# 16x16 blocks gathered on chip for a block inverse, and norm sums moved ahead of their products, in a hybrid decoder layer

## The chip, the cores and the metric

The kernel runs on one core of a Trainium2 chip. The metric is the device time of one execution in microseconds, as the median of several runs. A core has a matrix engine (TensorE, PE in the rows; PEld is its loading of the stationary operand), a vector engine (VectorE, DVE), an engine for functions and scaled copies (ScalarE, ACT), a general one (GpSimd, Pool), and a queue engine (SyncE, SP) that issues transfers. Every engine works its own instructions in order; they wait for one another through semaphores. A "q" behind an engine's name in a row is its sequencer, which waits or issues. Transfers are issued from SP, ACT and Pool.

## The reference

One layer on a sequence of 256 tokens, with 2048 channels. An input projection feeds three token mixers, their outputs are mixed and projected, and a SwiGLU FFN follows, each with a norm before and a norm after:

```
h = rms_norm(x, norm_mix_pre)
p = h @ w_in                                     # columns for three mixers and the merge gates
y_a = RG-LRU(p)     y_b = gated DeltaNet(p)      y_c = RWKV-7(p)
m = sum_b sigmoid(gate_b) * (y_b @ w_branch[b])
x = x + rms_norm(m @ w_out, norm_mix_post)
h = rms_norm(x, norm_ffn_pre)
x = x + rms_norm((silu(h @ w_gate) * (h @ w_up)) @ w_down, norm_ffn_post)
```

DeltaNet (8 heads, chunks of 64 tokens) and RWKV-7 (16 heads) are written in chunked form, and each chunk needs the inverse of a unit triangular 64x64 matrix.

## The kernel before

Products are made in three parts: each factor is split into a rounded high part and the rest, and high x high, high x low and low x high are added up. The weights arrive as tiles of 1 MB (`raw`, L203, issued from SP, three buffers); each half of one is cast to `wh` on ACT (L214) and the rest `wl = raw - wh` is made on DVE (L216), three buffers each; then TensorE multiplies (L241 to L243 or L262 to L264). The order of instructions on each engine is laid down before the run by a planner that simulates the engines; `high_priority` and `issue_after` steer it.

The mixers run in four quarters of 256 channels. A quarter `q` projects the slabs of RWKV (`rwkv_quarter`), of DeltaNet (`gdn_pair`) and of the LRU (`lru_quarter`). The first two make the triangular matrices of their chunks, `st` (L564, 1 MB) and `U` (L750, 0.25 MB), and hand them to `inverse64`, which works in steps:

- The 16x16 blocks on the diagonals are copied from SBUF to a DRAM tile `dblk`, with eight transfers issued from Pool (L381), one for each group of 16 partitions `r`.
- They come back in one transfer from Pool (L383) into the SBUF tile `B`, in which each of the 16 partitions of a group holds all the blocks of its group: 8 KB per partition for RWKV (`nu` = 8), 4 KB for DeltaNet (`nu` = 4), so 1 MB and 0.5 MB. The source has dimensions 8, 16 (repeated) and the row.
- `after = yield` returns to the caller, who goes on with DeltaNet and the LRU. When the LRU's last instruction (L867) is known, `xc` is set (L388) behind it, and a recurrence of 15 steps on DVE (L392, L393) inverts the 16x16 blocks out of `B`.
- Small products on TensorE join 16 to 32 and 32 to 64 (L410 to L435), and the rest of the mixer follows.

Meanwhile TensorE has the next quarter's projections. Behind the last quarter come the remaining gate blocks and `branch(0)`, whose inputs `yf`, `yh`, `yl` (L1030 to L1033) take buffers of the tag `u4`, which `B` of DeltaNet has too (there are six).

`product_a` makes the output projection and the last projection of the FFN, in four column blocks `j` for two halves `t` of the tokens. Each result is squared and summed on ACT (L1090) and multiplied by the norm's weight on DVE (L1091). Behind `product_a` the sums are reduced (L1105, L1167), `rstd` scales them on DVE (L296) and takes the power -1/2 on Pool (L297), and the residual is added: in `group` (L1110), and in the end for `j` < 3 on DVE (L1173), for `j` = 3 as a scaled copy on ACT (L1175) and an add on Pool (L1176); each part is then written out (L1177).

Of the kernel before, what the change touches and what calls it, by code (L numbers as in the profile page):

```python
# [8 lines left out]
F32 = mybir.dt.float32  # L9
# [5 lines left out]
P = 128  # L15
# [125 lines left out]
class Builder:  # L141
# [227 lines left out]
    def inverse64(self, nu, diag16, block, transposed):  # L369
# [4 lines left out]


        dd = self.dp.tile([8, nu, 16, 16], F32, name=self.uid("dblk"))
        for r in range(8):
            src = diag16(r)
            dst = dd[r].rearrange("(u n) j t -> j u n t", n=src.shape[2]) if len(src.shape) == 4 else \
                dd[r].rearrange("u j t -> j u t")  # L380
            nc.gpsimd.dma_start(dst, src)  # L381
        B = (self.u8 if nu == 8 else self.u4)("B").rearrange("p (u j t) -> p u j t", u=nu, j=16)
        nc.gpsimd.dma_start(B.rearrange("p u j t -> p (u j t)"),  # L383
                            dd.rearrange("r u j t -> r (u j t)").unsqueeze(1).to_broadcast([8, 16, nu * 256]))
# [72 lines left out]
    def rwkv_quarter(self, q, kS, rS, vS, up, y):  # L457
# [110 lines left out]
        X, = yield from self.inverse64(8, lambda r: st8[16 * r:16 * r + 16, :, (r < 4)::2, 16 * r:16 * r + 16],  # L568
# [128 lines left out]
    def gdn_pair(self, q_, qS, kS, vS, sz, y):  # L697
# [70 lines left out]
        J, JT = yield from self.inverse64(4, lambda r: h4(U)[16 * r:16 * r + 16, :, 16 * r:16 * r + 16],  # L768
# [103 lines left out]
def build(tc, aps, out):  # L872
# [209 lines left out]
    def product_a(w, ah, al, kts, hm, nw, ssq):  # L1082
        for j in range(4):
            b.ahead_evac = FIRST if j == 3 else None
            js = slice(j * 512, (j + 1) * 512)

            def sink(ps, j=j, js=js):
                for t in range(2):
                    junk = sp.tile([P, 512], F32, name=b.uid("junk"), tag="stage", bufs=b.stage_bufs)
                    nc.scalar.activation(junk, ps[t], AF.Square, accum_out=ssq[:, t, j:j + 1])  # L1090
                    nc.vector.tensor_tensor(hm[:, t, js], ps[t], nw[:, js], ALU.mult)  # L1091

            b.block_a(wp, pp, w[j], ah, al, kts, sink, j == 3)
        b.ahead_evac = None
# [3 lines left out]
    product_a(aps["w_out"], mh, ml, KD, hm, n2, ssq)  # L1098
    x1d = [b.dp.tile([P, D], F32, name=f"x1d{t}") for t in range(2)]
    xh, xl = acts("h")  # L1100
    with tc.high_priority(FIRST):
        tots = [fp.tile([P, 6], F32, name=f"tot{t}") for t in range(2)]
        r1 = []
        for t in range(2):
            nc.vector.tensor_reduce(tots[t][:, 0:1], ssq[:, t], AX.X, ALU.add)  # L1105
            r1.append(b.rstd(fp, tots[t][:, 0:1], 1, 1.0 / D, EPS))

        def group(t, k0):
            js = slice(k0 * P, (k0 + 4) * P)
            nc.vector.scalar_tensor_tensor(x1[t][:, js], hm[:, t, js], r1[t], x1[t][:, js], ALU.mult, ALU.add)  # L1110
            return x1[t][:, js]

        last = b.to_channels(pp, group, "n3", xh, xl)
# [49 lines left out]
    product_a(aps["w_down"], ah, al, KF, od, n4, ssq)  # L1163
    r4 = []
    for t in range(2):
        tot = ap_.tile([P, 1], F32, name=f"tot4{t}")
        nc.vector.tensor_reduce(tot, ssq[:, t], AX.X, ALU.add)  # L1167
        r4.append(b.rstd(ap_, tot, 1, 1.0 / D, EPS))
    for t in range(2):
        for j in range(4):  # L1170
            js = slice(j * 512, (j + 1) * 512)
            if j < 3:
                nc.vector.scalar_tensor_tensor(od[:, t, js], od[:, t, js], r4[t], x1[t][:, js], ALU.mult, ALU.add)  # L1173
            else:
                nc.scalar.activation(od[:, t, js], od[:, t, js], AF.Identity, scale=r4[t])  # L1175
                nc.gpsimd.tensor_tensor(od[:, t, js], od[:, t, js], x1[t][:, js], ALU.add)  # L1176
            (nc.sync, nc.scalar)[j % 2].dma_start(out[t * P:(t + 1) * P, js], od[:, t, js])  # L1177
# [22 lines left out]
```

## Time and profile before

| | us |
|---|---|
| time, median of 3 runs (1879.31 to 1880.51) | 1879.42 |
| profiled execution | 1879.03 |
| its span, first to last instruction | 1877.3 |
| TensorE busy | 1839.9 |
| DVE busy | 1114.8 |
| ACT busy | 850.5 |
| Pool busy | 82.6 |

The table's busy times are of the profiled execution. A matmul's end is modelled, so a stretch with TensorE busy throughout is one in which its queue did not run dry. The granted clock is a share of full speed (1.00 is 2.4 GHz, 0.50 is 1.2 GHz). The share of transfers is the mean busy share of the 16 transfer engines. In a row of the time line the columns are the start, the duration, the engine, the line of the program, the operation, what it writes and reads, the shapes, how many are merged into the row, and in brackets the idle time before it and what ended that.

### The profile page before, as it was taken

The page shows a single profiled execution, that of the slowest core. Times are in us where ns is not written, and L with a number is a line of the kernel's source. Part 1 is how long each engine was busy: PE and PEld are TensorE (multiplying, and loading weights), DVE is VectorE, ACT ScalarE, POOL GpSimd, SP SyncE. Part 2 cuts the span into 40 slices and gives each one's busy share as a digit, 9 for nine tenths or more (in the row PEclk, how much of TensorE's full clock was granted, in tenths as well). Part 3 has the DMA queues.
Part 4 walks back from the last instruction along what each step waited for, and adds up shares of the span by engine and source line. Part 5 has one row for each costly group of instructions (what it writes and reads, how often), then busy time and mean ns, then how long its engine had stood idle before and what let it go on. Part 6 is the DMA issues. An engine that isn't in the chain of part 4 may idle for free.

```text
span 1877.3 us, 27855 instructions
## 1 busy us (share of the span) xinstructions
PE 1839.9 (98%) x11516; PEld 1591.6 (85%) x11516; DVE 1114.8 (59%) x1622; ACT 850.5 (45%) x1055; POOL 82.6 (4%) x150
## 2 busy tenths in 40 slices
PE   9999999999999999899999999999999999999997
PEld 9999997999798988677888887888888888888886
DVE  6768667666776577656655556445545444444444
ACT  7445355434543465334444445444444444443442
POOL 0011010200120012000000000000000000000000
PEclk9999999999999999899999999999999999999999
DMA  7565445644565355648655556555555555555553
GB/s 263 183 183 200 141 152 189 169 162 153 178 168 175 134 183 174 202 164 310 209 194 183 195 186 234 194 196 184 194 187 191 191 181 199 204 200 188 194 200 114
DMA packets 61647, 352.06 MB, mean 188 GB/s; under 512 B 9040, under 2 KB 10832, under 8 KB 22480
## 3 DMA queue, kind: packets, MB, share of 16 engines
q1 hardware_dynamic: 50256, 327.18, 50.4%
q10 hardware_dynamic: 6752, 14.31, 2.1%
q0 software_dynamic: 4512, 8.79, 1.9%
q8 instruction: 90, 1.47, 0.3%
q14 instruction: 37, 0.30, 0.0%
HBM read 336.22 MB, written 14.02 MB: 187 GB/s over the span
## 4 chain that ended last, share of the span: by engine, by line
PE 53%; issue 38%; DMA 4%; DVE 3%; ACT 2%; POOL 1%; ACTq 0%; DVEq 0%; POOLq 0%; SPq 0%
PE mm L264 8%; PE mm L263 8%; PE mm L262 8%; PE mm L243 7%; PE mm L242 7%; PE mm L241 7%; DMA raw<-in_w_in_dram 2%; DVE wl L216 1%; DMA B<-dblk 1%; ACT wh L214 1%; PE psa L592 1%; PE pr L585 1%; PE pr L596 1%; PE px L562 0%; PE pst L602 0%
## 5 line engine op out<-in xcount | busy, mean ns | idle before, releaser
L216 DVE TENSOR_TENSOR wl<-raw,wh 128x1024 fp32r<-128x1024 f32 x590 | 720.9, 1223 | 616.8 <-ACT wh L214 614.6
L214 ACT CAST wh<-raw 128x1024 fp32r<-128x1024 f32 x590 | 620.1, 1052 | 856.9 <-PE mm L264 594.8
L241 PE MATMUL mm<-xh,wh 128*128 128x256 f32 x1200 | 344.4, 287 | 5.3 <-ACT wh L214 5.3
L243 PE MATMUL mm<-xh,wl 128*128 128x256 f32 x1200 | 344.9, 288 | 2.1 <-DVE wl L216 1.1
L242 PE MATMUL mm<-xl,wh 128*128 128x256 f32 x1200 | 345.0, 288 | 1.1 <-DVE xl L909 1.0
L263 PE MATMUL mm<-wl,hh 128*128 128x512 f32 x704 | 275.1, 391 | 0.5 <-DVE wl L216 0.5
L264 PE MATMUL mm<-wh,hl 128*128 128x512 f32 x704 | 274.8, 390 | 0.0
L262 PE MATMUL mm<-wh,hh 128*128 128x512 f32 x704 | 250.7, 392 | 2.0 <-DVE rstd L296 1.5
L241 PEld LDWEIGHTS mm<-xh,wh 128*128 128x128 f32 x1200 | 232.2, 194 | 7.5 <-ACT wh L214 6.0
L243 PEld LDWEIGHTS mm<-xh,wl 128*128 128x128 f32 x1200 | 231.9, 193 | 3.9 <-DVE wl L216 1.7
L242 PEld LDWEIGHTS mm<-xl,wh 128*128 128x128 f32 x1200 | 232.1, 193 | 2.4 <-DVE xl L909 1.5
L262 PEld LDWEIGHTS mm<-wh,hh 128*128 128x128 f32 x704 | 132.3, 188 | 29.4 <-ACT hh L311 2.5
L263 PEld LDWEIGHTS mm<-wl,hh 128*128 128x128 f32 x704 | 132.7, 189 | 27.8 <-DVE wl L216 0.7
L264 PEld LDWEIGHTS mm<-wh,hl 128*128 128x128 f32 x704 | 132.6, 188 | 27.5
L263 PE MATMUL mm<-wl,xh 128*128 128x512 f32 x384 | 151.0, 393 | 1.2 <-DVE wl L216 1.1
L264 PE MATMUL mm<-wh,xl 128*128 128x512 f32 x384 | 150.2, 391 | 0.0
L262 PE MATMUL mm<-wh,xh 128*128 128x512 f32 x384 | 139.5, 392 | 0.0
L263 PE MATMUL mm<-wl,ah 128*128 128x512 f32 x352 | 137.0, 389 | 0.0
L264 PE MATMUL mm<-wh,al 128*128 128x512 f32 x352 | 136.9, 389 | 0.0
L262 PE MATMUL mm<-wh,ah 128*128 128x512 f32 x352 | 123.5, 389 | 0.0
L297 POOL TENSOR_TENSOR rstd<-rstd,mhalf 128x8 f32<-128x8 f32 (+3 forms) x23 | 29.7, 1295 | 1453.7 <-DVE rstd L296 1453.7
L263 PEld LDWEIGHTS mm<-wl,xh 128*128 128x128 f32 x384 | 72.1, 188 | 17.8 <-DVE wl L216 2.5
(294 smaller groups left out, 2023.8 us busy)
## 6 DMA issues: line engine op xcount, KB each, us to landing
raw<-in_w_in_dram SPq DMA_DIRECT2D x72, 1024.0 KB, 4.9
raw<-in_w_mix_dram SPq DMA_DIRECT2D x48, 1024.0 KB, 4.9
raw<-in_w_gate_dram SPq DMA_DIRECT2D x44, 1024.0 KB, 4.9
raw<-in_w_up_dram SPq DMA_DIRECT2D x44, 1024.0 KB, 4.8
raw<-in_w_down_dram SPq DMA_DIRECT2D x44, 1024.0 KB, 4.9
raw<-in_w_branch_dram SPq DMA_DIRECT2D x24, 1024.0 KB, 4.9
raw<-in_w_out_dram SPq DMA_DIRECT2D x16, 1024.0 KB, 4.8
keep<-stage ACTq DMA_DIRECT2D x24, 256.0 KB, 5.2
```

What stands on the lines that cost most here:

```text
L214: nc.scalar.copy(wh[:, :n], s)
L216: nc.vector.tensor_tensor(wl[:, :n], s, wh[:, :n].bitcast(F32), ALU.subtract)
L241: nc.tensor.matmul(o, hs, xh[:, k], start=(k == 0 and c == 0), stop=False, skip_group_check=True)
L242: nc.tensor.matmul(o, hs, xl[:, k], start=False, stop=False, skip_group_check=True)
L243: nc.tensor.matmul(o, ls, xh[:, k], start=False, stop=(k == kts - 1), skip_group_check=True)
L262: nc.tensor.matmul(ps[t], xh[:, k, ts], h, start=(k == 0), stop=False)
L263: nc.tensor.matmul(ps[t], xh[:, k, ts], l, start=False, stop=False)
L264: return nc.tensor.matmul(ps[t], xl[:, k, ts], h, start=False, stop=(k == kts - 1))
L297: nc.gpsimd.tensor_tensor(r, r, self.mhalf.to_broadcast([P, n]), ALU.pow)
L585: nc.tensor.matmul(pq[bb, us], st[u][:, n, bb], sav[:, n, us], start=not n, stop=True, skip_group_check=True)
L592: nc.tensor.matmul(ps[bb, us], X[bb, 2 * u + p], R[bb, us], start=True, stop=True)
L596: nc.tensor.matmul(pq[ob, us], st[u][:, n, ob], sav[:, n, us], start=not n, stop=True, skip_group_check=True)
```

## The change

Three things are edited.

- `inverse64` no longer issues eight transfers. For each quarter of the partitions (32, two groups of 16) ACT copies the left block columns, multiplied by a 0/1 mask of the partitions, into an SBUF tile `C`, and DVE adds the right block columns times the other mask. One transfer from Pool writes `C` to `dblk`, and `B` is read from there, with the block's row `j` now ahead of the unit `u`. `C` uses the buffers of the tag that the recurrence's `xt` has.
- `product_a` takes a function `rms`, called for the last column block between the square and the weight product, that reduces the sums and makes `rstd`; both callers hand in theirs.
- At the end both the third and the fourth column block are scaled on ACT, and all four adds are on DVE; nothing is added on Pool.

```diff
@@ -366,22 +366,28 @@
             nc.vector.scalar_tensor_tensor(out[:, c], out[:, c], mu(c), s[:, c, 1:257], ALU.mult, ALU.add)
 
 
-    def inverse64(self, nu, diag16, block, transposed):
+    def inverse64(self, nu, diag, block, transposed):
 
 
 
         nc, mp, n = self.nc, self.mp, nu * 32
 
-        dd = self.dp.tile([8, nu, 16, 16], F32, name=self.uid("dblk"))
-        for r in range(8):
-            src = diag16(r)
-            dst = dd[r].rearrange("(u n) j t -> j u n t", n=src.shape[2]) if len(src.shape) == 4 else \
-                dd[r].rearrange("u j t -> j u t")
-            nc.gpsimd.dma_start(dst, src)
-        B = (self.u8 if nu == 8 else self.u4)("B").rearrange("p (u j t) -> p u j t", u=nu, j=16)
-        nc.gpsimd.dma_start(B.rearrange("p u j t -> p (u j t)"),
-                            dd.rearrange("r u j t -> r (u j t)").unsqueeze(1).to_broadcast([8, 16, nu * 256]))
+        def like(t, a):
+            return t.rearrange("p (u n) t -> p u n t", n=a.shape[2]) if len(a.shape) == 4 else t
+        C = mp.tile([P, nu, 16], F32, name=self.uid("C"), tag=f"xt{nu}", bufs=2)
+        for i in range(4):
+            qs = slice(32 * i, 32 * i + 32)
+            nc.scalar.activation(like(C[qs], diag(i, 0)), diag(i, 0), AF.Copy, scale=self.cst("blk16", 0, 1)[qs])
+            nc.vector.scalar_tensor_tensor(like(C[qs], diag(i, 1)), diag(i, 1), self.cst("blk16", 16, 1)[qs],
+                                           like(C[qs], diag(i, 1)), ALU.mult, ALU.add)
+        dd = self.dp.tile([P, nu * 16], F32, name=self.uid("dblk"))
+        nc.gpsimd.dma_start(dd, C.rearrange("p u t -> p (u t)"))
+        B = (self.u8 if nu == 8 else self.u4)("B")
+        nc.gpsimd.dma_start(B, dd.rearrange("(r j) n -> r (j n)", j=16).unsqueeze(1).to_broadcast([8, 16, nu * 256]))
+        B = B.rearrange("p (j u t) -> p u j t", u=nu, j=16)
         after = yield
         xc = mp.tile([P, nu, 16], F32, name=self.uid("xc"), tag=f"xc{nu}", bufs=1)
         with self.tc.issue_after(after):
@@ -565,7 +571,8 @@
                                         ps[h].rearrange("p (m e s) -> p m e s", m=2, e=2), mask, ALU.mult)
 
 
-        X, = yield from self.inverse64(8, lambda r: st8[16 * r:16 * r + 16, :, (r < 4)::2, 16 * r:16 * r + 16],
+        X, = yield from self.inverse64(8, lambda i, h: st8[32 * i:32 * i + 32, :, (i < 2)::2,
+                                                               32 * i + 16 * h:32 * i + 16 * h + 16],
                                        lambda h, w: st[w // 2][64 * h:64 * h + 64, 2 * (w % 2) + (h < 1),
                                                                64 * h:64 * h + 64], False)
 
@@ -765,7 +772,7 @@
             nc.scalar.activation(kd[:, i], h4(ps)[:, i], AF.Copy, scale=h4(dm)[:, 2 * i, P - 1:P])
 
 
-        J, JT = yield from self.inverse64(4, lambda r: h4(U)[16 * r:16 * r + 16, :, 16 * r:16 * r + 16],
+        J, JT = yield from self.inverse64(4, lambda i, h: h4(U)[32 * i:32 * i + 32, :, 32 * i + 16 * h:32 * i + 16 * h + 16],
                                lambda h, u: h4(U)[64 * h:64 * h + 64, u, 64 * h:64 * h + 64], True)
         lo_, hi = slice(0, 64), slice(64, 128)
         v64 = lambda t: t[:, 0:256].rearrange("p (u t) -> p u t", t=64)
@@ -1079,7 +1086,8 @@
         x1.append(fp.tile([P, D], F32, name=f"x1_{t}"))
         nc.scalar.dma_start(x1[t], aps["x"][t * P:(t + 1) * P])
 
-    def product_a(w, ah, al, kts, hm, nw, ssq):
+    def product_a(w, ah, al, kts, hm, nw, ssq, rms):
         for j in range(4):
             b.ahead_evac = FIRST if j == 3 else None
             js = slice(j * 512, (j + 1) * 512)
@@ -1088,6 +1096,8 @@
                 for t in range(2):
                     junk = sp.tile([P, 512], F32, name=b.uid("junk"), tag="stage", bufs=b.stage_bufs)
                     nc.scalar.activation(junk, ps[t], AF.Square, accum_out=ssq[:, t, j:j + 1])
+                    if j == 3:
+                        rms(t)
                     nc.vector.tensor_tensor(hm[:, t, js], ps[t], nw[:, js], ALU.mult)
 
             b.block_a(wp, pp, w[j], ah, al, kts, sink, j == 3)
@@ -1095,16 +1105,17 @@
 
     hm = fp.tile([P, 2, D], F32, name="hm")
     ssq = fp.tile([P, 2, 4], F32, name="ssq")
-    product_a(aps["w_out"], mh, ml, KD, hm, n2, ssq)
+    tots = [fp.tile([P, 6], F32, name=f"tot{t}") for t in range(2)]
+    r1 = []
+    def rms1(t):
+        nc.vector.tensor_reduce(tots[t][:, 0:1], ssq[:, t], AX.X, ALU.add)
+        r1.append(b.rstd(fp, tots[t][:, 0:1], 1, 1.0 / D, EPS))
+    product_a(aps["w_out"], mh, ml, KD, hm, n2, ssq, rms1)
     x1d = [b.dp.tile([P, D], F32, name=f"x1d{t}") for t in range(2)]
     xh, xl = acts("h")
     with tc.high_priority(FIRST):
-        tots = [fp.tile([P, 6], F32, name=f"tot{t}") for t in range(2)]
-        r1 = []
-        for t in range(2):
-            nc.vector.tensor_reduce(tots[t][:, 0:1], ssq[:, t], AX.X, ALU.add)
-            r1.append(b.rstd(fp, tots[t][:, 0:1], 1, 1.0 / D, EPS))
         def group(t, k0):
             js = slice(k0 * P, (k0 + 4) * P)
             nc.vector.scalar_tensor_tensor(x1[t][:, js], hm[:, t, js], r1[t], x1[t][:, js], ALU.mult, ALU.add)
@@ -1160,21 +1171,25 @@
     n4 = full(xp, "n4", aps["n4"], tag="xl")
     od = xp.tile([P, 2, D], F32, name="od", tag="xh")
     ssq = ap_.tile([P, 2, 4], F32, name="ssq2")
-    product_a(aps["w_down"], ah, al, KF, od, n4, ssq)
     r4 = []
-    for t in range(2):
+    def rms4(t):
         tot = ap_.tile([P, 1], F32, name=f"tot4{t}")
         nc.vector.tensor_reduce(tot, ssq[:, t], AX.X, ALU.add)
         r4.append(b.rstd(ap_, tot, 1, 1.0 / D, EPS))
+    product_a(aps["w_down"], ah, al, KF, od, n4, ssq, rms4)
     for t in range(2):
-        for j in range(4):
-            js = slice(j * 512, (j + 1) * 512)
-            if j < 3:
-                nc.vector.scalar_tensor_tensor(od[:, t, js], od[:, t, js], r4[t], x1[t][:, js], ALU.mult, ALU.add)
+        o = [od[:, t, j * 512:(j + 1) * 512] for j in range(4)]
+        x = [x1[t][:, j * 512:(j + 1) * 512] for j in range(4)]
+        for j in (3, 2):
+            nc.scalar.activation(o[j], o[j], AF.Identity, scale=r4[t])
+        for j in (0, 1, 3, 2):
+            if j < 2:
+                nc.vector.scalar_tensor_tensor(o[j], o[j], r4[t], x[j], ALU.mult, ALU.add)
             else:
-                nc.scalar.activation(od[:, t, js], od[:, t, js], AF.Identity, scale=r4[t])
-                nc.gpsimd.tensor_tensor(od[:, t, js], od[:, t, js], x1[t][:, js], ALU.add)
-            (nc.sync, nc.scalar)[j % 2].dma_start(out[t * P:(t + 1) * P, js], od[:, t, js])
+                nc.vector.tensor_tensor(o[j], o[j], x[j], ALU.add)
+            (nc.sync, nc.scalar)[j % 2].dma_start(out[t * P:(t + 1) * P, j * 512:(j + 1) * 512], o[j])
     while b.cp:
         b.drop()
```

## Rows read from the trace of the kernel before

**Rows 1.** The page: busy time of TensorE; the casts of weights on ACT.
```profile
PE 1839.9 (98%) x11516; PEld 1591.6 (85%) x11516; DVE 1114.8 (59%) x1622; ACT 850.5 (45%) x1055; POOL 82.6 (4%) x150
...
L214 ACT CAST wh<-raw 128x1024 fp32r<-128x1024 f32 x590 | 620.1, 1052 | 856.9 <-PE mm L264 594.8
```

**Rows 2.** Stretches: PE, PEld, DVE, ACT, POOL busy us; clock, transfer share, GB/s.
```profile
188.00:235.00 47.00, 47.00 (x675) 45.05 (x675) 29.46 (x85) 18.09 (x28) 0.00 (x0) 1.00 0.41 140
341.00:353.00 12.00, 12.00 (x100) 11.43 (x99) 9.34 (x15) 7.36 (x13) 8.98 (x17) 1.00 0.14 32
353.00:377.00 24.00, 21.36 (x176) 20.88 (x174) 15.66 (x30) 7.14 (x7) 0.60 (x1) 0.99 0.98 217
372.00:385.00 13.00, 10.04 (x59) 9.56 (x59) 8.93 (x31) 4.08 (x4) 0.00 (x0) 0.74 0.77 247
567.00:580.00 13.00, 9.53 (x57) 9.03 (x57) 8.31 (x29) 4.08 (x4) 0.00 (x0) 0.74 0.73 240
776.00:800.00 24.00, 18.08 (x377) 15.30 (x376) 12.75 (x53) 7.97 (x19) 0.00 (x0) 0.57 0.37 131
```

**Rows 3.** Time line of ACT and DVE, 374 to 378 us.
```profile
374.96 1.99 ACT L214 CAST wh<-raw 128x1024 fp32r<-128x1024 f32 x2 [8.65 <-DMA raw<-in_w_in_dram]
...
376.03 1.23 DVE L216 TENSOR_TENSOR wl<-raw,wh 128x1024 fp32r<-128x1024 f32 x1 [5.59 <-ACT wh L214]
```

**Rows 4.** Landing times, medians of the page; last, the weight load issued at 357.0.
```profile
raw<-in_w_in_dram SPq DMA_DIRECT2D x72, 1024.0 KB, 4.9
B<-dblk POOLq DMA_DIRECT2D x4, 1024.0 KB, 21.5
dblk<-U POOLq DMA_DIRECT2D x32, 4.0 KB, 2.4
...
DMA to landing us min/median/max: 17.8/17.8/17.8
```

**Rows 5.** Time line of Pool in the second and the fourth quarter.
```profile
343.43 4.10 POOL L381 DMA_DIRECT2D dblk<-U  x8 [28.86 <-DVE U L750]
...
351.80 0.62 POOL L383 DMA_DIRECT2D B<-dblk  x1
353.55 0.60 POOL L383 DMA_DIRECT2D B<-dblk  x1 [1.13 <-DMA dblk<-st]
...
742.38 4.17 POOL L381 DMA_DIRECT2D dblk<-st  x8 [1.04 <-DVE st L564]
...
748.41 0.60 POOL L383 DMA_DIRECT2D B<-dblk  x1 [1.25 <-DMA dblk<-st]
```

**Rows 6.** Instruction groups by shape: busy us and mean ns of one.
```profile
L437 ACT ACTIVATE XT<-px 32x128 f32<-32x128 f32 x8 | 2.1, 268 | 0.2
...
L611 DVE SCALAR_TENSOR_TENSOR S<-S,pc,cst_t 128x128 f32<-128x128 f32 x16 | 5.0, 345 | 0.1
```

**Rows 7.** Time line of DVE, 344 to 346 us.
```profile
344.60 1.29 DVE L564 TENSOR_TENSOR st<-px,cst_t 128x512 f32<-128x512 f32 x2 [0.54 <-PE px L562]
```

**Rows 8.** Time line of DVE and ACT, fourth quarter.
```profile
763.36 1.23 DVE L216 TENSOR_TENSOR wl<-raw,wh 128x1024 fp32r<-128x1024 f32 x1 [5.46 <-ACT wh L214]
...
779.37 1.05 ACT L1032 CAST yh<-yf 128x1024 fp32r<-128x1024 f32 x1 [1.16 <-DVE xt L392]
```

**Rows 9.** Time line of DVE between output projection and FFN.
```profile
1126.51 0.68 DVE L1091 TENSOR_TENSOR hm<-mm,n 128x512 f32<-128x512 f32 x1
...
1128.11 2.74 DVE L1110 SCALAR_TENSOR_TENSOR x<-hm,rstd,x 128x512 f32<-128x512 f32 x4 [0.67 <-POOL rstd L297]
```

**Rows 10.** Time line of DVE and ACT at the end.
```profile
1866.22 0.68 DVE L1091 TENSOR_TENSOR od<-mm,n 128x512 f32<-128x512 f32 x1
1866.82 0.14 DVE L1167 TENSOR_REDUCE tot<-ssq 128x1 f32<-128x4 f32 x1
...
1867.80 3.08 DVE L1173 SCALAR_TENSOR_TENSOR od<-od,rstd,x1r 128x512 f32<-128x512 f32 x3 [0.66 <-POOL rstd L297]
...
1865.82 0.19 ACT L1090 ACTIVATION_READ_ACCUMULATOR junk<-mm 128x1 f32 x1
```

## Prediction

> **What bounds the kernel now.** I read the page first. TensorE is busy for 1839.9 us of the span of 1877.3 [rows 1], so all that an edit can win is TensorE's idle time and the stretches in which its clock is low. Next I cut the span into stretches and read busy time and granted clock of each. In the first quarter's inverse TensorE has no idle time at all and the full clock, 2.4 GHz (188 to 235 us) [rows 2]. In the second and third quarter there is one hole each: 13 us hold 10.04 and 9.53 us of TensorE's work, at a mean clock of 0.74, so the clock was at its lower level (1.2 GHz) for 2 x 0.26 x 13 = 6.8 us [rows 2]. In the fourth (776 to 800) TensorE is busy 18.08 of 24 us at a mean clock of 0.57 [rows 2]. The other idle places are the passage between the output projection and the FFN, and the end.
>
> Then the waits: what made the hole of the second quarter? ACT waited 8.65 us for a weight tile from DRAM before two casts (L214), and DVE stood 5.59 us behind that cast although the inverse's recurrence (L392) was queued right after [rows 3]. So the hole is late weights. The transfers say why: a weight load of 1 MB lands in 4.9 us as a rule, the one issued at 357.0 took 17.8; the copy into B, also 1 MB, takes 21.5 [rows 4]. From 341 to 353 us the transfer engines are all but idle, share 0.14, and from 353 to 377 full, 0.98, at 217 GB/s [rows 2]. Pool's queue gives the order: U is there at 343.43, its eight gathers take 4.10 us to issue, the eight of st follow, and only then the two copies into B go out, at 351.80 and 353.55 [rows 5], into the time of the next weight loads. The gathers hold the B copies back through the idle time.
>
> **The change, part by part.** (a) The gather of the 16x16 blocks. Removed per inverse: seven of eight Pool issues, 8 inverses x 7 x 0.51 us (4.10 / 8 [rows 5]) = 29 us of Pool's time; on the path only the B copies are queued behind them. Added per inverse: four masked copies on ACT and four multiply-adds on DVE, each on 32 partitions of 128 or 64 elements, and one transfer on Pool. ACT's scaled copy of 32x128 took 0.27 us, DVE's three-operand form of 128x128 0.35 [rows 6]: 1.1 and 1.4 us per inverse, 8.6 and 11 us in all. In 188 to 235 us DVE is busy 29.5 and ACT 18.1 of 47 us while TensorE is full [rows 2], so I price these at nothing: TensorE's products cover them. Without that cover each inverse would cost 4 x 0.27 + 0.35 = 1.4 us.
>
> When do the B copies start? ACT's copies run ahead of DVE's adds, so the tile C stands 4 x 0.27 + 0.35 = 1.4 us after its source; then 0.5 us of issue and 2.4 of landing, the row of U's gathers [rows 4]: 4.3 us. U is there at 343.4 [rows 5]: its B copy goes out at 347.7 instead of 351.80. st is there at 345.9 [rows 7]: 350.2 instead of 353.55, 3.3 us earlier. If ACT is then in a cast (1.0 us) and DVE in a subtraction (1.2 us) [rows 3], it is 1.1 us earlier; those are the ends, and I take 3.3, since DVE has a gap of 0.54 us just there [rows 7].
>
> What does it give? The load that landed at 374.8 us (357.0 + 17.8 [rows 4]) stopped TensorE. It comes 3.3 us earlier by the shift. The 0.5 MB copy of U is also out of the crowded time then: 0.5 MB at 217 GB/s [rows 2] is 2.4 us more. TensorE lacked 13 - 10.04 = 2.96 us [rows 2], so 5.7 us of advance closes the hole with 2.7 to spare; the low end (1.1 + 2.4 = 3.5) just closes it too. Without the idle time I expect the clock to stay at 2.4 GHz, as in 188 to 235 us [rows 2]. Worth in the second quarter: 2.96 us idle, and half of the 6.8 us at 1.2 GHz, less some 0.75 of it that were idle: (6.8 - 0.75) / 2 = 3.0, together **6.0 us**. Third quarter: 3.47 idle and (6.8 - 1.1) / 2 = 2.8 [rows 2]: **6.3 us**. The first has no hole: nothing.
>
> Fourth quarter. st is there only at 742.4 and its copy goes out at 748.41 [rows 5]; afterwards at 742.4 + 4.3 = 746.7, 1.7 earlier, so this copy still meets weight loads. TensorE here is not short of weights alone: at the end of its idle time the cast of yh (L1032) waits for a buffer that the recurrence on B gives back, and the recurrence began behind a DVE subtraction that had waited 5.46 us for late weights [rows 8]. The weights come 1.7 + 2.4 = 4.1 us earlier by the same sum, and the chain behind with them: **4.1 us**. Its ends: 0, if the collision stays, and 5.5, the whole wait [rows 8]; with the clock full from 776 to 800 (2 x 0.43 x 24 = 20.6 us at 1.2 GHz [rows 2]) up to 10 more, which I leave out because TensorE's work there is a chain of small products with gaps.
>
> The Trainium skill, page "DMA: Bandwidth & Descriptors", section "Rules for kernel authors", says that a transfer whose outermost dimension is under 16 is confined to that many of the 16 engines. B's source begins with a dimension of 8 in both kernels. B's 21.5 us beside 4.9 for the same megabyte [rows 4] agrees, though other traffic is in that row. By this rule the costly copy stays as it is and only moves; that is the first rival.
>
> (b) Sums ahead of products at L1090. Between projection and FFN the second half's product into hm (L1091) starts on DVE at 1126.51, the reduction comes behind it, and the first residual add (L1110) at 1128.11 [rows 9]. Now the reduction goes first, and the product runs while Pool takes the power. One product holds the reduction for 0.60 us (1866.22 to 1866.82 at the end, which has the same pair [rows 10]): **0.6 us**. The ends are 0.3, if the product then stands before the add, and 0.7.
>
> (c) The end. Now: product 1866.22, reduction 1866.82, first of three adds 1867.80, and with Pool's add beside them the three take 3.08 us, to 1870.9 [rows 10]. Four adds without Pool took 2.74 [rows 9]. Pool's adds go, and DVE does four per half. The last sum is read at 1866.01 [rows 10]; the first half's adds, 0.6 us earlier and without Pool's company, are off DVE by then. From there 0.98 us to the first add, as from 1866.82 to 1867.80 [rows 10], and 2.74: 1869.7 instead of 1870.9, **1.1 us** with 0.1 for the hand-over. ACT's scaled copies go beside the first two adds. The ends are 0.4 and 1.4: an issue on ACT may stand before the square.
>
> The new order inside B (j before u) leaves the innermost run contiguous and L392's counts alike: nothing, under the cover named.
>
> Sum: 6.0 + 6.3 + 4.1 + 0.6 + 1.1 = 18.1 us. The profiled execution took 1879.03 us around its span of 1877.3; that gives 1860.9, and the median of the runs lies 0.4 above: **1861 us**.
>
> **The rivals.** *The collision only moves.* The B copies start 1 to 2 us earlier, since the masked copies wait behind casts and subtractions, and the weights still come late. For it: in the fourth quarter st itself is late [rows 5]; against it: twelve microseconds at share 0.14 [rows 2]. Then only (b) and (c) stay: 1879.4 - 1.7 = 1877.7 us. Chance 0.13.
>
> *The fourth quarter opens too.* 5.5 instead of 4.1, and 6 of the 10 us of low clock: 1861 - 1.4 - 6 = 1853.6 us. For it: the first quarter runs the same chain at full clock [rows 2]; against it: after 776 us few weight products are left to fill the gaps. Chance 0.14.
>
> *Slower: ACT is held.* ACT works in order. A masked copy that waits for U or st at the head of ACT holds the weight cast behind it, and DVE's add waits for ACT and holds the subtraction; DVE stood 5.59 us in that way [rows 3]. Place: 343 to 348 us and its likes, in all four quarters. It decides once ACT is held for longer than the split weights in stock last, three halves of some 3.2 us (590 casts in the span [rows 1]). Then a hole of 6 us stays in two quarters and appears in the two others: 1879.4 + 2 x 6 - 1.7 = 1890 us. Against it: the producers are done within some 2 us of each other [rows 5, 7]. Chance 0.07.
>
> **How the numbers follow.** The forecast has 0.66. On the low side the range takes in the better rival, with the ends of (b) and (c) and some of the remaining clock: 1849 us; on the high side one of the two holes kept and nothing from the fourth quarter: 1861 + 6.3 + 4.1 = 1871.4, 1872 us. Left out are the rival in which the collision only moves and the slower one, 0.20. Changes within 0.2% (3.8 us) can't be told from none here: faster by more 0.66 + 0.14 = 0.80, within 0.13, slower 0.07.
>
> **What would show it.** The B copy of st issued near 350 us, B's landing under 15 us; no wait of ACT for weights over 4 us in the middle quarters; TensorE full and at full clock where the two 13 us stretches are; the reduction ahead of hm's product; no Pool add at the end, and the last DVE add 1.1 us sooner after TensorE's last product. I am wrong if weight loads beside B still take 13 us and more, if casts stand behind masked copies that wait, or if the order of TensorE's work around the inverse is another one.

## The result, and the profile after

The changed kernel takes 1891.72 us (median of 4 runs, 1889.15 to 1892.20), the kernel before on the same chip 1879.37. The ratio is 1.0063, with a 95% interval of 1.0045 to 1.0080: **slower by 0.6%**, where 1861 us and faster was forecast.

| us | after |
|---|---|
| profiled execution, its span | 1889.15, 1887.4 |
| TensorE busy | 1840.8 |
| DVE, ACT, Pool busy | 1121.3, 864.4, 51.1 |

TensorE's work is the same (1839.9 before [rows 1]); the span is 10.1 us longer. To see where, one can match the 8880 weight products of both traces one by one and take the difference of their starts. After the first quarter's inverse they lag by 0.7 us, after the second's by 4.7, the third's 5.7, the fourth's 14.1; behind the passage to the FFN by 13.6; and the span ends 10.1 later. So in these two traces the gather costs 14.1 us, and the norm edits give 4.0 back. Such lags move by some 1 us from trace to trace where nothing was edited (norms_alone gains 1.2 us in the third quarter), so smaller differences of theirs say nothing.

What TensorE waits for has changed as well. Its first and third product of a weight tile, on the page of the kernel before and then on that of the kernel after:

```profile
L241 PE MATMUL mm<-xh,wh 128*128 128x256 f32 x1200 | 344.4, 287 | 5.3 <-ACT wh L214 5.3
L243 PE MATMUL mm<-xh,wl 128*128 128x256 f32 x1200 | 344.9, 288 | 2.1 <-DVE wl L216 1.1
```

```profile
L241 PE MATMUL mm<-xh,wh 128*128 128x256 f32 x1200 | 344.0, 287 | 0.0
L243 PE MATMUL mm<-xh,wl 128*128 128x256 f32 x1200 | 343.5, 287 | 13.0 <-DVE wl L216 13.0
```

Before, it waited for casts of late weights; after, for the weight subtractions on DVE.

The stretches of the holes in the kernel after (columns as in [rows 2]):

```profile
341.00:353.00 12.00, 12.00 (x98) 11.34 (x97) 10.05 (x23) 8.91 (x20) 1.78 (x3) 1.00 0.24 79
353.00:377.00 24.00, 16.84 (x137) 16.43 (x136) 14.61 (x24) 7.61 (x8) 0.61 (x1) 0.98 0.73 195
366.00:379.00 13.00, 7.28 (x51) 7.07 (x51) 4.22 (x15) 2.09 (x2) 0.00 (x0) 0.88 0.66 187
565.00:578.00 13.00, 7.51 (x49) 7.31 (x48) 6.17 (x22) 1.94 (x3) 0.00 (x0) 0.74 0.57 163
768.00:800.00 32.00, 20.05 (x301) 15.78 (x300) 20.78 (x80) 9.16 (x11) 0.00 (x0) 0.83 0.59 207
```

The last of them in the kernel before:

```profile
768.00:800.00 32.00, 25.54 (x407) 20.84 (x406) 19.83 (x79) 12.18 (x23) 0.00 (x0) 0.68 0.46 164
```

The two 13 us stretches of the second and third quarter hold 7.28 and 7.51 us of products instead of 10.04 and 9.53 [rows 2], and 768 to 800 loses 5.5. In the idle time before, 341 to 353 us, the transfer share is 0.24 instead of 0.14: something was moved there, but the crowd behind it stayed. What was moved shows Pool's time line, second and fourth quarter:

```profile
346.19 0.61 POOL L387 DMA_DIRECT2D dblk<-C  x1 [32.59 <-DVE C L384]
349.01 0.61 POOL L389 DMA_DIRECT2D B<-dblk  x1 [2.21 <-PE mm L243]
349.62 0.56 POOL L387 DMA_DIRECT2D dblk<-C  x1
356.30 0.61 POOL L389 DMA_DIRECT2D B<-dblk  x1 [6.11 <-DMA dblk<-C]
...
746.88 0.61 POOL L389 DMA_DIRECT2D B<-dblk  x1 [3.20 <-PE px L855]
748.28 0.56 POOL L387 DMA_DIRECT2D dblk<-C  x1 [0.79 <-DVE C L384]
756.96 0.60 POOL L389 DMA_DIRECT2D B<-dblk  x1 [8.12 <-DMA dblk<-C]
```

U's copy into B goes out 2.8 us sooner than before, but st's goes out at 356.30 instead of 353.55, and at 756.96 instead of 748.41 [rows 5]. Before, both gathers stood ahead of both copies. Now U's copy slips in ahead of st's small write, and that write lands 6.4 us after its issue instead of some 2. The chain that ends with DVE's first step of the recurrence reads it off:

```profile
349.62 6.39 DMA dblk<-C
356.01 0.29 issue
356.30 18.39 DMA B<-dblk
374.78 0.06 DVE xt L398
```

The second thing is the order on DVE. The recurrence's first step waits for B at the head of the queue, with the weight subtractions behind it. DVE's time line:

```profile
364.77 0.68 DVE L341 TENSOR_TENSOR slab<-mm,rbc 128x512 f32<-128x512 f32 x1
374.78 0.41 DVE L398 TENSOR_TENSOR xt<-B,xc 128x120 f32<-128x120 f32 x2 [9.33 <-DMA B<-dblk]
375.12 1.22 DVE L216 TENSOR_TENSOR wl<-raw,wh 128x1024 fp32r<-128x1024 f32 x1
...
773.75 0.41 DVE L398 TENSOR_TENSOR xt<-B,xc 128x120 f32<-128x120 f32 x2 [10.81 <-DMA B<-dblk]
```

ACT's, with the cast whose subtraction waits there and the one that comes behind the fourth quarter's wait:

```profile
367.46 1.05 ACT L214 CAST wh<-raw 128x1024 fp32r<-128x1024 f32 x1 [1.82 <-PE mm L242]
...
781.75 1.05 ACT L214 CAST wh<-raw 128x1024 fp32r<-128x1024 f32 x1 [12.80 <-DVE xc L399]
```

The cast of 367.46 is done at 368.5; its subtraction waits until 375.12 behind a step that has nothing to do with it. In the kernel before, DVE had waited for the cast (5.59 us [rows 3]), and the recurrence stood behind. The planner orders by its own simulated times, and put the first step ahead; that it did so because the blocks are ready earlier there is likely, but no run shows it. In the fourth quarter ACT's next cast has to wait 12.80 us in turn.

### The profile page after: what moved, and what is told of

Read it like the earlier page. It is cut to its first block, busy times and chain, and to the rows that moved or that the text cites. A ratio compares the mean times of both kernels' runs of the same rounds, so it can differ in the third digit from the quotient of the medians.

```text
span 1887.4 us, 27814 instructions
## 1 busy us (share of the span) xinstructions
PE 1840.8 (98%) x11516; PEld 1591.8 (84%) x11516; DVE 1121.3 (59%) x1656; ACT 864.4 (46%) x1089; POOL 51.1 (3%) x92
## 4 chain that ended last, share of the span: by engine, by line
PE 90%; DMA 5%; DVE 2%; issue 1%; ACT 1%; POOL 0%; ACTq 0%; POOLq 0%; DVEq 0%; SPq 0%
PE mm L263 21%; PE mm L264 21%; PE mm L262 21%; PE mm L242 6%; PE mm L243 6%; PE mm L241 6%; DMA B<-dblk 3%; DMA dblk<-C 1%; DMA raw<-in_w_in_dram 1%; PE tp L285 1%; PE pr L592 1%; PE pr L603 1%; PE psa L599 1%; PE px L568 1%; DVE wl L216 1%
## 5 line engine op out<-in xcount | busy, mean ns | idle before, releaser
L263 PEld LDWEIGHTS mm<-wl,xh 128*128 128x128 f32 x384 | 72.7, 189 | 26.7 <-DVE wl L216 10.1
L262 PEld LDWEIGHTS mm<-wh,xh 128*128 128x128 f32 x384 | 72.6, 189 | 17.9 <-issue 1.7
```

Source lines behind the costliest of these rows:

```text
L262: nc.tensor.matmul(ps[t], xh[:, k, ts], h, start=(k == 0), stop=False)
L263: nc.tensor.matmul(ps[t], xh[:, k, ts], l, start=False, stop=False)
```

## The experiments

All twelve runs against the kernel before on the same chip; the last column is the ratio times 1879.4 us, less 1879.4.

| run | median us | ratio (95%) | us against before |
|---|---|---|---|
| (the change) | 1891.72 | 1.0063 (1.0045 to 1.0080) | +11.8 |
| norms_alone | 1875.20 | 0.9981 (0.9972 to 0.9990) | -3.6 |
| dve_order | 1872.12 | 0.9962 (0.9947 to 0.9977) | -7.1 |
| writes_first | 1877.37 | 0.9995 (0.9986 to 1.0005) | -0.9 |
| both_orders | 1868.42 | 0.9945 (0.9930 to 0.9960) | -10.3 |
| copies_unused | 1884.91 | 1.0032 (1.0020 to 1.0044) | +6.0 |
| before_eager | 1889.64 | 1.0054 (1.0037 to 1.0071) | +10.1 |
| write_on_act | 1892.93 | 1.0073 (1.0058 to 1.0088) | +13.7 |
| three_orders | 1872.15 | 0.9965 (0.9952 to 0.9978) | -6.6 |
| wide_after | 1863.09 | 0.9921 (0.9903 to 0.9938) | -14.8 |
| two_writes | 1891.17 | 1.0061 (1.0044 to 1.0078) | +11.5 |
| wide_orders | 1861.89 | 0.9912 (0.9894 to 0.9930) | -16.5 |
| wide_recip | 1858.53 | 0.9897 (0.9882 to 0.9912) | -19.4 |

**norms_alone.** The kernel before, with `product_a`'s `rms` and the end of the change, and the old `inverse64`.

> The kernel before with the two norm edits alone (sums ahead of products, no Pool adds at the end); the gather is the old one with eight transfers. In the trace of after TensorE's products gain 0.54 us on before's between the output projection and the FFN (their lag falls from 14.13 to 13.59 us), and the span ends 8.9 us behind TensorE's last product instead of 12.4. Theory: these two gains are the norm edits' own and add up: 1879.4 - 0.5 - 3.5 = 1875.4 us. Rival: they are worth what I predicted, 0.6 and 1.1, and the rest of the 3.5 is noise of one profile: 1877.7 us.

Measured -3.6 us: the theory's sum, but not both of its parts. The products' lag shows where: the passage gives nothing in this run (-1.29 us ahead of it, which came in the third quarter where nothing was edited, -1.18 behind), and the end gives 3.2.

**dve_order.** Of the change one thing is undone, the order on DVE: an edge for the order of issue, without a wait, from the weight subtraction of before's place to the first step.

```diff
-                    nc.vector.tensor_tensor(wl[:, :n], s, wh[:, :n].bitcast(F32), ALU.subtract)
+                    sub = nc.vector.tensor_tensor(wl[:, :n], s, wh[:, :n].bitcast(F32), ALU.subtract)
+                for step, rank in self.held:
+                    if rank == self.subs - self.base:
+                        tc.add_manual_dep(step, sub.ins.name, ...)
+                self.subs += 1
...
```

(`held` has the first steps of a quarter's recurrences, each with the number of the subtraction that it stood behind before.) The planner then moves more around that edge: some 300 of DVE's 1656 instructions stand elsewhere than in the kernel after.

> The changed kernel, with one thing undone: on DVE the first step of each recurrence is queued behind the same weight subtraction as in the kernel before (order only, no new wait; Pool's queue stays as in after, so the copy into B stays as late). Theory one (DVE's queue holds the subtractions): the first step no longer stands at the head of DVE for 9.33, 9.10 and 10.81 us with subtractions behind it; TensorE's holes near 373, 570 and 773 us, 5.7, 5.5 and 8.8 us, shrink to about those of before (3.0, 3.5, 5.1), and the low clock behind them shrinks too: 8 to 11 us less than after, 1881 to 1884 us. Theory two (the late copy into B itself delays weights and the chain behind): B is as late as in after, the holes stay within 2 us each: 1889 to 1892 us.

Measured 1872.1 us, 19 us less than after (1.0063 to 0.9962), about twice the 8 to 11 of theory one. st's copy goes out just as late (357.55 us), and nobody waits for it in the second quarter; DeltaNet's steps (128x60) run, DVE waits for a cast as in the kernel before, and st's first step (128x120) stands behind:

```profile
366.43 1.23 DVE L220 TENSOR_TENSOR wl<-raw,wh 128x1024 fp32r<-128x1024 f32 x1 [0.21 <-ACT wh L218]
367.57 0.21 DVE L407 TENSOR_TENSOR xt<-B,xc 128x60 f32<-128x60 f32 x1
...
377.96 1.22 DVE L220 TENSOR_TENSOR wl<-raw,wh 128x1024 fp32r<-128x1024 f32 x1 [6.12 <-ACT wh L218]
379.11 0.38 DVE L407 TENSOR_TENSOR xt<-B,xc 128x120 f32<-128x120 f32 x2
```

The two 13 us stretches hold 11.45 and 10.70 us of products, more than before (10.04 and 9.53), where theory one had them come back to before's. That is a part of why it gives more; the rest wasn't separated.

**before_eager.** The reverse: before's kernel with the subtraction queued behind the first steps.

```diff
+                if self.quarter is not None and self.subs - self.base == EAGER[self.quarter]:
+                    for step in self.held:
+                        tc.add_manual_dep(sub.ins, step.name, ...)
...
```

> The kernel before with one thing of after put in: on DVE the weight subtraction that stood ahead of the recurrences is queued behind their first steps, as the planner ordered it in after. Gather, copies and transfers are before's. Theory (the order on DVE alone costs time, since the first step waits for B at the head of the queue): TensorE's holes near 373 and 569 us grow from 3.0 and 3.5 to 5 us and more, and the one near 770 as well: 5 to 10 us slower than before, 1884 to 1889 us. Rival (the order costs only where the copy into B is late as in after): within 2 us of before, 1877 to 1881 us.

Measured +10.1 us, the upper end of the theory; the rival is out. The old gather with the new order has the same wait, and three subtractions behind it:

```profile
379.02 0.28 DVE L401 TENSOR_TENSOR xt<-B,xc 128x120 f32<-128x120 f32 x1 [8.70 <-DMA B<-dblk]
379.22 3.49 DVE L220 TENSOR_TENSOR wl<-raw,wh 128x1024 fp32r<-128x1024 f32 x3
```

But this run isn't the pinned pair alone, since the planner rearranged more behind it: TensorE's longest idle time here, 8.08 us, ends with a cast that had waited 8.2 us for weights, and only 1.75 us end with a subtraction. What part of the 10 us is the subtraction's isn't shown.

**writes_first.** Only Pool's order is undone.

```diff
+        with self.tc.issue_after(other) if other else contextlib.nullcontext():
+            nc.gpsimd.dma_start(B, ...)
```

(`other` is st's write, for U's copy.) This edit is clean: only four of DVE's instructions change places, and SP's none.

> The changed kernel, with one thing undone: on Pool the copy into B of U is queued behind the write of st's blocks, as the gathers stood ahead of both copies before. DVE's planned order stays as in after. Theory one (the small write lies behind the 0.5 MB copy on Pool's own queue of transfers): st's write lands in about 2.3 us instead of 6.5, st's copy into B goes out near 352 us instead of 356.3 and near 751 instead of 757.0; the wait of DVE's first step falls by 4 us in the second and 5 in the fourth quarter, nothing in the third, where the write waited for its data: about 1883 us. Rival (the write is slow because the transfer engines are full of weights): the write still takes over 5 us, both copies go out later: 1892 us or more.

Measured 1877.4 us, 13 us less than after, more than the 9 of the theory. st's copy goes out at 352.52 and 751.83. In the third quarter, as expected, st's copy goes out no sooner against the products: its write waits for its data there, since DVE's reciprocal (3.35 us) stands ahead of the last masked add.

**both_orders.** The two together.

> Both of the other two edits together: before's order on Pool (both writes, then both copies) and before's order on DVE (first steps behind the same subtractions). If order on the two queues is the whole loss, the masked copies cost next to nothing and the transfers start about 1.4 us earlier than before in the second quarter: before's time less the norm edits, 1875 us, or a little under. If the masked copies cost by themselves (they hold the LRU's chain on ACT and DVE by 2.4 us in the second quarter), some 1.5 us are lost in each of three quarters: 1880 us. If neither order matters: 1891 us.

Measured 1868.4: lower than the lowest theory. TensorE is at full clock and holds 12.24 of 13 us in the second quarter and 11.06 in the third; from 768 to 800 it holds 26.67 of 32 at a clock of 0.68. Pool's rows:

```profile
346.79 0.61 POOL L396 DMA_DIRECT2D dblk<-C  x1 [32.59 <-DVE C L393]
350.22 0.55 POOL L396 DMA_DIRECT2D dblk<-C  x1 [2.82 <-DVE C L393]
350.76 0.63 POOL L401 DMA_DIRECT2D B<-dblk  x1
352.51 0.61 POOL L401 DMA_DIRECT2D B<-dblk  x1 [1.12 <-DMA dblk<-C]
```

The gains of the two orders (19 and 13 us) don't add up; both end the same wait.

**copies_unused.** The kernel before, with the masked copies into `C` added and read by nobody.

> The kernel before with the masked copies added on ACT and DVE, but nothing reads them: the gathers and both copies into B are the old ones, and on DVE the recurrences stay behind the same weight subtractions. It prices the copies by themselves. My prediction priced them at nothing: 1878.7 us, as before. Theory: they push the LRU's gate chain and with it the reciprocal (3.35 us on DVE) 2.4 us back, and the weight subtraction that is queued behind the reciprocal comes too late for TensorE: holes as in the changed kernel, 0.4 us near 134, 1.4 near 354, 0.9 near 753, with lags of 1.3, 1.7 and 1.6 us. Where the late weights stop TensorE afterwards anyway (near 373) some of the lag is taken up: 1880 to 1883 us. The upper end is every inverse without cover, 4 x 1.4 us: 1884 us.

Measured 1884.9 us, +6.0, just above the upper end that the theory named, every inverse without cover. One copy of st took 0.40 us on ACT in the kernel after, one add 0.34 on DVE. Both push the LRU's reciprocal back, and with it the subtraction behind it. DVE's time line before, then with the copies:

```profile
349.12 3.35 DVE L859 RECIPROCAL rec<-rec 128x512 f32<-128x512 f32 x1
352.39 1.16 DVE L216 TENSOR_TENSOR wl<-raw,wh 128x1024 fp32r<-128x1024 f32 x1
```

```profile
350.94 3.35 DVE L871 RECIPROCAL rec<-rec 128x512 f32<-128x512 f32 x1
354.21 1.16 DVE L216 TENSOR_TENSOR wl<-raw,wh 128x1024 fp32r<-128x1024 f32 x1
```

1.8 us later on DVE; and the stretch of 353 to 357 us with the copies (columns as in [rows 2]):

```profile
353.00:357.00 4.00, 2.56 (x22) 2.36 (x21) 4.00 (x4) 1.77 (x2) 0.61 (x1) 1.00 0.69 158
```

TensorE stands idle for 1.44 of these 4 us. The hole comes in the third quarter too; by the lag the copies cost 2.2, 2.5 and 3.1 us in the second to the fourth quarter and nothing in the first.

**write_on_act.** Is Pool's queue of transfers what holds the small write?

```diff
-        nc.gpsimd.dma_start(dd, C.rearrange("p u t -> p (u t)"))
+        nc.scalar.dma_start(dd, C.rearrange("p u t -> p (u t)"))
```

> The changed kernel, with the two small writes of the blocks issued from ACT instead of Pool; the copies into B stay on Pool, DVE's order stays as in after. In the second quarter the write of st's blocks is then issued while U's copy into B is under way, as in after, but on another queue of transfers. Theory (a queue works its transfers one behind the other, and the small write lay behind the copy): the write lands in about 2.3 us, st's copy goes out near 352 us instead of 356.3 and near 751 instead of 757.0; about the time of the run with both writes first, 1877 us. Rival (the transfer engines are taken up by U's copy, whatever queue the write comes from): the write takes 5 us and more as in after, and the time is after's, 1890 us.

Measured 1892.9 us: the theory falls. From ACT's queue the write lands in 7.0 us, from Pool's in 6.4 (fourth quarter: 10.6 and 8.4). U's copy holds it, not the queue that it shares.

ACT's time line, then Pool's:

```profile
350.60 0.33 ACTq L387 DMA_DIRECT2D dblk<-C  x1
```

```profile
357.92 0.58 POOL L389 DMA_DIRECT2D B<-dblk  x1 [8.02 <-DMA dblk<-C]
```

**three_orders.** both_orders, with the reciprocal queued behind the subtraction that had stood behind it, and behind the last masked add.

> The kernel of the run with both orders, with a third order put in: on DVE the LRU's reciprocal is queued behind the one weight subtraction that stood right behind it (in the first, second and fourth quarter), and behind the last masked add (third quarter). Theory (the masked copies cost through the subtraction that is stuck behind the reciprocal): the holes of 0.4, 1.4 and 0.9 us near 134, 355 and 742 us go, and with them lags of 1.3, 1.7 and 1.6 us; in the third quarter st's copy into B goes out some 3 us sooner. 1868.4 - 4.6 = 1864 us. Rival (the copies cost because ACT makes the casts late): the holes stay, 1868 us.

Measured 1872.2, 4 us more than both_orders (0.9965 to 0.9945, with intervals that just overlap): neither theory. The hole near 355 shrank (1.44 to 0.78 us, now at 358, and ended by a cast, as the rival had it) and so did the fourth quarter's lag, but the third quarter got worse, because st's copy went out sooner: at 544.70 instead of 547.70. That is ahead of the weight load of 546.74 instead of behind it, and the loads of that time then landed in 13.3 us at least instead of 9.7.

SP's time line, then ACT's:

```profile
546.74 8.84 SPq L208 DMA_DIRECT2D raw<-in_w_in_dram  x3
```

```profile
563.77 1.99 ACT L219 CAST wh<-raw 128x1024 fp32r<-128x1024 f32 x2 [9.80 <-DMA raw<-in_w_in_dram]
```

An earlier copy catches one more load. That load, issued 2.0 us behind the copy, landed at 563.67 us, 0.6 behind the copy (544.70 + 18.37 = 563.07). So the shift that my sum counted on is no gain by itself: the load lands when the copy has landed.

**wide_after, two_writes.** That leaves the copy itself. In `wide_after` the blocks are written twice, so that the copy's source begins with 16; in the control they are written twice too, and read as before.

```diff
-        dd = self.dp.tile([P, nu * 16], F32, name=self.uid("dblk"))
-        nc.gpsimd.dma_start(dd, C.rearrange("p u t -> p (u t)"))
+        dd = self.dp.tile([8, 2, 16, nu * 16], F32, name=self.uid("dblk"))
+        for a in range(2):
+            write = nc.gpsimd.dma_start(dd[:, a], C.rearrange("p u t -> p (u t)")).ins
...
-        nc.gpsimd.dma_start(B, dd.rearrange("(r j) n -> r (j n)", j=16).unsqueeze(1).to_broadcast([8, 16, nu * 256]))
+        nc.gpsimd.dma_start(B, dd.rearrange("r a j n -> (r a) (j n)").unsqueeze(1).to_broadcast([16, 8, nu * 256]))
```

> The changed kernel, with one thing changed: the blocks are written to DRAM twice (a second small write from Pool), so that the source of the copy into B begins with a dimension of 16 (repeated 8 times) instead of 8 (repeated 16 times); what lands in B is the same. All orders are after's. Theory (the copy is slow because it runs on few transfer engines, and the 1 MB weight loads wait behind it on those): its median landing falls from 18.4 us to 10 or less, DVE's first step waits 9.3, 9.1 and 10.8 us less some 8 each, TensorE's holes of 5.7, 5.5 and 8.8 us go nearly, 1876 to 1880 us in spite of the order on DVE. The Trainium skill, page DMA: Bandwidth & Descriptors, section Rules for kernel authors, says that an outermost dimension of 16 spreads over all 16 engines. Rival (the landing is set by the traffic as a whole, at some 220 GB/s): it lands in 15 us and more, 1889 to 1893 us.

> The control to the run with the wider source: the blocks are written to DRAM twice as there, but the copy into B reads from the second of them with the old shape, 8 rows repeated 16 times. All orders are the planner's. Theory (the shape of the source made the wider copy faster): the copy into B lands in some 18 us again, DVE's first steps wait for it at the head of the queue, 1889 to 1895 us. Rival (the second write, by shifting the start of the copy, or another order of the planner made the gain): 1863 to 1870 us.

Measured 1863.1 us, 13 less than the theory gave, and 1891.2 as it gave. (The 18.4 us in the first expectation is the second quarter's copy; the median of after's four is 17.2.) The landing of the 1 MB copy, on the pages of two_writes and of wide_after:

```profile
B<-dblk POOLq DMA_DIRECT2D x4, 1024.0 KB, 17.7
```

```profile
B<-dblk POOLq DMA_DIRECT2D x4, 1024.0 KB, 10.1
```

The weight loads issued from 352 to 372 us, in the same order:

```profile
DMA to landing us min/median/max: 4.9/13.9/16.2
```

```profile
DMA to landing us min/median/max: 9.0/9.7/11.2
```

The stretches of the holes in wide_after:

```profile
366.00:379.00 13.00, 12.99 (x108) 12.79 (x108) 10.40 (x41) 4.78 (x6) 0.00 (x0) 1.00 0.65 238
565.00:578.00 13.00, 13.00 (x115) 12.87 (x117) 12.11 (x47) 4.20 (x4) 0.00 (x0) 1.00 0.55 193
768.00:800.00 32.00, 30.55 (x417) 25.21 (x417) 16.23 (x36) 14.98 (x32) 1.04 (x1) 1.00 0.38 126
```

No order is pinned here, the same bytes land in B, and all three holes are gone (1.45 us of small gaps remain in the last stretch; the hole near 354 of the masked copies stays). The two runs have the same instructions in the same order on DVE, ACT, Pool and SP, so the shape of the source alone is worth 1.0061 less 0.9921, 26 us. Of the 1 MB copy's packets at most 9 to 11 are under way at once in two_writes, and 16 to 19 in wide_after. The Trainium skill's page "DMA: Bandwidth & Descriptors", section "Rules for kernel authors", says that an outermost dimension under 16 confines a transfer to at most that many engines; the two runs agree (17.7 and 10.1 us).

**wide_orders, wide_recip.** The wide source with both orders pinned, and with the reciprocal's place alone.

> The kernel of the run with both orders, with the same wider source for the copy into B. Theory (few engines): the weight loads that are issued beside the copy land in 8 us or less, the holes left near 371 and 567 us (0.8 and 1.9 us) go, and in the fourth quarter the recurrence begins some 5 us sooner: 1868.4 - 4 to 8 = 1860 to 1864 us. Rival (the traffic as a whole sets the landing): 1868 us, or up to 2 us more for the second write.

> The kernel with the wider source (all else as in after), and the LRU's reciprocal on DVE queued behind the last masked add and behind the one weight subtraction that stood right behind it. Theory (the masked copies cost through that subtraction, and the copy into B no longer collides with the weight loads): the holes of 1.4 and 2.0 us near 354 and 735 us go, with lags of 1.7 and some 3 us: 1858 to 1860 us. Rival (as in the run with three orders, an earlier copy into B catches one more weight load and takes the gain back): 1862 to 1866 us.

1861.9 and 1858.5 us, both as the theory said. With the wide copy the orders are worth next to nothing (1863.1 and 1861.9, overlapping intervals). The reciprocal's place gives some 4.5 us (0.9921 to 0.9897), what it could not give with the narrow one; these intervals overlap by a little too, but the trace bears it out: the hole near 354 shrinks from 1.44 to 0.78 us, and that of 2.03 us near 735 is gone. wide_recip beats both kernels: 1.0% under before.

## Why the prediction was wrong

**What bounds it** was right for the kernel before: late weights behind the copies into B, and TensorE waiting for their casts.

**The failed step** is the sentence in which the load "comes 3.3 us earlier by the shift". It failed in three ways; in the kernel after that load was issued at 359.44 us and landed at 374.60, where the sum had 371.5. First, st's copy did not go out at 350.2 us but at 356.3: its write was given "the row of U's gathers" as landing, 2.4 us [rows 4], a row with no copy in flight, and I kept before's order on Pool without saying so. Second, the shift was taken as a gain by itself; three_orders shows that it isn't, since the loads issued behind the copy wait for it wherever it stands. Third, I kept before's order on DVE, again without saying so. There the first step of the recurrence now stands ahead of the subtractions and waits 9.33, 9.10 and 10.81 us for B; with before's order on DVE the late copy costs far less (dve_order, 19 us under after), with before's order on Pool that wait is shorter (writes_first, 13 us under). Of the signs, "weight loads beside B still take 13 us and more" came (15.2 and 12.8 in the second quarter).

**The rival with the rule** (*the collision only moves*) named the cause: B's source begins with 8 in both kernels. It got 0.13, and 1877.7 us, because I let twelve idle microseconds speak against it and took a copy that moves as harmless. What it lacked was the order: a copy that moves late, with DVE's subtractions behind it.

**Removed from Pool**: right, 82.6 us busy became 51.1, and off the path, as priced.

**The masked copies** were priced at nothing, and cost 6.0 us (copies_unused). The cover that I named, TensorE's products, was there, but by 1.4 us too thin: DVE's reciprocal came 1.8 us later and TensorE stood idle for 1.44, since one subtraction stands behind that 3.35 us reciprocal, and it behind the copies. I looked at busy shares (DVE 29.5 of 47 us [rows 2]) where the slack of one chain decides. One term was also too small: 0.40 us for each copy on ACT instead of 0.27 [rows 6]; DVE's 0.34 was right.

**The quarters' gains** (6.0, 6.3 and 4.1). With both orders back, and the copies' cost still in, the matched products gain 3.0, 3.8 and 1.6 us; in wide_recip 4.8, 5.8 and 5.5. So the idle time was there to be won, in about that size, by another edit than the one I priced.

**The slower rival** (ACT is held, 1890 us) has the right time for the wrong reason: ACT's masked copies waited 2.5 us at most; DVE was held, by B. My sign for this, "casts stand behind masked copies that wait", did not come. No sign named DVE's order, though [rows 3] showed the recurrence right behind a subtraction.

**(b)** forecast 0.6; the lag shows 0.5 in the change, -0.1 in norms_alone, 1.0 in both_orders. The reduction does go first, but the planner put the product between it and the scaling, so the first add starts 1.48 us after the reduction (1.00 before):

```profile
1140.63 0.15 DVE L1112 TENSOR_REDUCE tot<-ssq 128x1 f32<-128x4 f32 x1
1140.70 0.68 DVE L1101 TENSOR_TENSOR hm<-mm,n 128x512 f32<-128x512 f32 x1
1141.30 0.14 DVE L296 TENSOR_SCALAR rstd<-tot 128x1 f32<-128x1 f32 x1
1142.11 2.74 DVE L1121 SCALAR_TENSOR_TENSOR x<-hm,rstd,x 128x512 f32<-128x512 f32 x4 [0.67 <-POOL rstd L297]
```

Of 0.6 us of advance 0.48 is lost again. What is left is less than the lags resolve: copies_unused, which has before's norms, gains 0.9 at the same place. So no run shows a gain of (b).

**(c)** forecast 1.1, measured 3.5 (13.6 less 10.1). From the last sum read to the end of the last add it is 4.12 us (1879.22 to 1883.34) instead of 4.87 [rows 10]: 0.75 of the 1.1. The square starts 0.04 us behind the last product instead of 0.42, another 0.4; together they are the 1.1 us that were the sign. The remaining 2.4 lie behind the last output transfer: from its issue to the end of the span 4.0 us instead of 6.4, though it lands in 2.8 and 2.7 at most. norms_alone has it too, so it comes with these edits, the Pool adds among them; no row shows what ends there. All runs with the norm edits gain 2.8 to 3.5 us from the last product to the end of the span, the two without (copies_unused, before_eager) nothing. So the 1.1 came by the path that was forecast, and the 2.4 were not in the sum.

**Left open**: why the pinned kernels lose less than before in the second and third quarter although their copy is as narrow. Fewer and larger gather transfers and an earlier start came together in them. And no run gives the kernel before the wide source, so what the gather on chip is worth by itself isn't shown.

## What to carry to other kernels

Look first at the shape of a slow transfer, not at its place: 16 rows ahead instead of 8 gave 26 us here, while moving the narrow copy gave 13 us at best, where a queue waited for it (writes_first), and cost time in three_orders. In a kernel whose instruction order is planned, an edit that makes one input seem ready sooner also reorders the in-order engines; compare the queue of each engine before pricing anything, and ask for each moved instruction what waits behind it. A price of nothing for small instructions needs the slack of the chain that they stand in, not the busy share of the engine.

## What the runs showed of the hardware

- A write of 64 KB lands in 6.4 us when it is issued on Pool 0.6 us behind a 0.5 MB copy, and in 7.0 when ACT issues it 1.4 us behind one; issued ahead of both copies it takes 2.0 (all in the second quarter, the last in both_orders).
- The same 1 MB into the same tile lands in 17.7 us from a source of 8 rows repeated 16 times and in 10.1 from one of 16 rows repeated 8 times, beside the same weight loads; at most 9 to 11 of its packets are under way at once in the first case, 16 to 19 in the second.
- The weight loads beside it land more evenly then, in 9.0 to 11.2 us instead of 4.9 to 16.2 (second quarter, three loads each); the median of all of them is 4.9 [rows 4].
- In the three stretches of the holes the granted clock was 0.88, 0.74 and 0.83 in the kernel after and 1.00 in wide_after: with the holes gone these stretches ran at 2.4 GHz.
